# Early FFN weights in separate buffers, and another share-out of the low parts between VectorE, ScalarE and DMA

## The chip, the cores and the metric

One core of one Trainium2 chip runs the whole kernel. The metric is the time of one execution in microseconds of device time; the kernel before has a median of 1083.88 us over three runs. Every core has TensorE (PE, matrix products), VectorE (DVE), ScalarE (ACT), GpSimd (POOL) and SyncE (SP), each with its own instruction queue that is worked off in order, and DMA queues. Here SP issues the loads of weights, POOL issues the DMAs that add to their destination, ACT issues a few stores and loads of attention.

## What is computed

A hybrid encoder of two layers on 512 tokens of width 1024. Layer 0 mixes the tokens with a bidirectional gated linear attention (GLA), layer 1 with grouped-query softmax attention with 2-D rotary positions. Each is followed by a gated MLP with a width-3 convolution in it. Cut to what matters here:

```python
for i in range(DEPTH):                      # DEPTH = 2
    h = rmsnorm(x, norm_mix[i])
    x = x + (gla_mixer(h, ...) if i % 2 == 0 else attn_mixer(h, ...))
    x = x + conv_ffn(rmsnorm(x, norm_ffn[i]), ffn_w_up[i], ffn_w_conv[i], ffn_b_conv[i], ffn_w_down[i])

def conv_ffn(h, w_up, w_conv, b_conv, w_down):
    u = h @ w_up                            # 1024 -> 2 x 2816
    u = depthwise_conv3(u, w_conv) + b_conv
    val, gate = jnp.split(u, 2, axis=-1)
    return (jax.nn.silu(gate) * val) @ w_down
```

## The kernel before

**Two parts of each number.** All matrix products run on float32 numbers that are rounded to a shorter format (fp32r). So that nothing is lost, each operand is split into a high part (hi, the rounded number) and a low part (lo = number - hi), and each product is three matmuls: hi x hi, hi x lo and lo x hi. Every weight piece (128 x 1024 numbers, 512 KB) therefore goes through three steps: SP loads it into a `raw` buffer, ScalarE rounds it into `wh`, and VectorE subtracts to get `wl` (`split`, tiles `wh<-raw` on L353 and `wl<-raw,wh` on L354). A second way relieves VectorE (`low_dma`): ScalarE copies the raw piece into `wh` (L303) and a second time, times -1, into `wl` (L304), and rounds it on the way, so that `wl` is -hi; then POOL issues a DMA that adds the full number from memory (L342, in `flush`), so that `wl` becomes number - hi. A product that uses the piece waits for that DMA. Which pieces go which way is set by tables: `LOW_0` (up chunks whose first piece has its low part made by DMA), `STRIP_0` (the same for strips of the down projection), `Q_DMA` (pairs of activations).

**The FFN.** The 2816 hidden features are cut in 22 chunks of 128 (times value and gate). Chunks 4 to 21 (`SEVEN`) use a scheme of seven products instead of eight blocks (`seven_up`), in which some operands are sums of weight quarters. Such a chunk has four pieces h = 0 to 3 (`summed`). Piece 0 is loaded as it is; of the others, piece 2 (`e`, the `sum` tile) is a sum of quarters, made by VectorE (L324) from two loaded strips, or, for the chunks in `SUMS_DMA`, by a load and an accumulating DMA (`total`). The first matmul of a chunk that uses the low part of piece 0 is the row `r<-nh,wl`. The down projection comes in two parts, begun at chunks 9 and 17 (`DOWN_AFTER`), each with four strips of four pieces, and in a tail. `prepare` rounds and splits the activations of two neighbouring chunks, pair p (pair 6 is chunks 12 and 13), into four `gu` tiles; this runs some chunks behind TensorE, pair 6 while TensorE is at chunk 15.

**Order and buffers.** The instructions of each engine stand in the order that a scheduler gives them by priority, and a list of weight pieces (`W.todo`) decides what is loaded and rounded next. `W.ahead` and `W.piece` take from its front. Raw pieces go in a ring of five buffers (`NR`), `wh` and `wl` in rings of four. A larger set of buffers (`big`, 22 of them, shared with tiles of the mixers and the FFN) also exists. The first three up chunks of each layer (`EARLY`, six pieces) are rounded while the mixer before still works: the loop `early` calls `W.ahead(1)` at the steps of the output projection listed in `EARLY_AT`; their `wh` and `wl` lie in `big` buffers, their raw in the ring. In layer 1 those steps lie at the end of attention, where the last head's output is copied (`oT<-po`, hi on ACT L1465, lo on DVE L1466) and projected (`op<-oT,wh`, L578), and VectorE adds the result to `x` (L586).

Of the kernel before, what the change touches and what calls it, by code (L numbers as in the profile page):

```python
# [8 lines left out]
F32 = mybir.dt.float32  # L9
F32R = mybir.dt.float32r  # L10
U8 = mybir.dt.uint8
AF = mybir.ActivationFunctionType
# [3 lines left out]
S = 512  # L16
# [57 lines left out]
EARLY = 3  # L74
TOKENS_AT = (0, 4)
ROOT_AT = (1, 1)
EARLY_AT = (16, 17, 18, 20, 22, 24, 26, 28), (18, 19, 20, 22, 24, 26, 28, 30)
RANK = 0
PA = 4
LOADS = 3  # L80
SWITCH = 3
INPUT_AT = {1: (0, 1), 2: (2, 3)}
Q_DMA = (6,)
UP_DMA = (3,)
SUMS_DMA = (14, 15, 16)
SUMS_NEAR = 6
LOW_0 = (5, 6, 7, 8, 9, 15, 16, 17)
LOW_1 = ()
LOW_2 = ()
STRIP_0 = (0, 4, 8)  # L90
# [1 line left out]
NR = 5  # L92
# [19 lines left out]
def hybrid_encoder_kernel(  # L112
# [23 lines left out]
    pe, act, dve, pool, sync = nc.tensor, nc.scalar, nc.vector, nc.gpsimd, nc.sync  # L136
# [9 lines left out]
    def nm(s):  # L146
        uid[0] += 1
        return f"{s}{uid[0]}"
# [40 lines left out]
    class Weights:  # L189
# [2 lines left out]

        def __init__(self):
            self.todo, self.made, self.by_dma, self.pending = [], {}, [], []
            self.sums, self.last, self.fine = set(), None, []
            self.loaded, self.strip, self.vg, self.totals = {}, {}, {}, {}
            self.loads, self.wide, self.turn = LOADS, 0, 0

# [36 lines left out]
        def fetch(self, src, i, h):  # L235
            key = (id(src), i, h)
            if key in self.loaded:
                return self.loaded.pop(key)
            t = pair("raw", NR, F32, "raw")
            n = 2 if any(src is a and i < m for a, m in self.fine) else 1  # L240
            for q in range(n):
                w = 2 * S // n
                sync.dma_start(t[:, q * w : (q + 1) * w], src[i, :, h * 2 * S + q * w : h * 2 * S + (q + 1) * w])
            return t

        def load(self, key):
            src, i, h = key
# [17 lines left out]
        def make(self, key):  # L265
            src, i, h = key
            if i < 0:
                self.made[id(src), i, h] = self.make_vg(src, -i, h)
                return
            self.load(key)  # L270
            if (id(src), i) in self.sums:
                self.made[id(src), i, h] = self.summed(src, i, h)
                return
            r = self.loaded.pop((id(src), i, h))
            if i < EARLY and any(src is a for a in up):
                hi, lo = big(F32R, "wh"), big(F32R, "wl")
            else:
                hi, lo = self.two()
            if any(src is a and i < n for a, n in self.by_dma):
                self.low_dma(hi, lo, r)  # L280
            elif any(src is a and i in UP_DMA for a in up):
                self.low_dma(hi, lo, r, src[i, :, h * 2 * S : (h + 1) * 2 * S].bitcast(F32R))
            else:
                self.split(hi, lo, r, 2 if src is w_first else 1, src is w_first and i == 0 and h == 0)
            self.made[id(src), i, h] = (hi, lo)
# [4 lines left out]
        def total(self, src, i):  # L290
            if i in (SUMS_DMA if any(src is a for a in up) else TAIL_SUMS) and (id(src), i) not in self.totals:
                self.totals[id(src), i] = e = big(F32, "sum")
                sync.dma_start(e, src[i, :, : 2 * S])
                self.pending.append((e, src[i, :, S : 3 * S]))
# [5 lines left out]
            return pair("wh", NH, F32R, "wh"), pair("wl", NL, F32R, "wl")  # L300

        def low_dma(self, hi, lo, r, home=None):
            act.activation(hi, r, AF.Copy)  # L303
            act.activation(lo, r, AF.Copy, scale=-1.0)  # L304
            self.pending.append((lo, r if home is None else home))

        def summed(self, src, i, h):


            tiles = self.strip[id(src), i]  # L310
            r, t3, e = tiles if h == 0 else [tiles[h % 3]] + tiles[1:]
            if h == 3:
                del self.strip[id(src), i]
                r = t3[:, S:]
                dve.tensor_tensor(r, r, t3[:, :S], ALU.add)
                hi, lo = (sp.tile([P, S], F32R, tag="sq", bufs=3, name=nm(a)) for a in ("wh4", "wl4"))
                act.activation(hi, r, AF.Copy)
                self.last = dve.tensor_tensor(lo, r, hi.bitcast(F32), ALU.subtract)
                return hi, lo
            if h == 1:  # L320
                with tc.issue_after(self.last.ins) if self.last else ExitStack():
                    if e is None:
                        tiles[2] = e = pair("raw", NR, F32, "sum")
                        dve.tensor_tensor(fold(e), t3[:, :S].rearrange("p (o n) -> p o n", o=1).to_broadcast([P, 2, S]),  # L324
                                          fold(tiles[0]), ALU.add)
                    dve.tensor_tensor(t3[:, :S], e[:, S:], tiles[0][:, :S], ALU.add)
                tiles[0] = None
            hi, lo = self.two()
            low = (LOW_0, LOW_1, LOW_2) if any(src is a for a in up) else (STRIP_0, (), STRIP_2)
            if i in low[h]:  # L330
                self.low_dma(hi, lo, r)
                if h == 0:
                    self.pending[-1] = (fold(lo), self.outer(src, i).bitcast(F32R))
            else:
                self.split(hi, lo, r)
            return hi, lo
# [40 lines left out]
    W = Weights()  # L377
    up = [w_up[i] for i in range(2)]
    down_w = [w_down[i] for i in range(2)]

    def add_up(layer, chunks):
        for m in chunks:
            W.add(up[layer], (m,), 4 if m in SEVEN else 2)
            if m in SEVEN and m - 1 not in SEVEN and m - 1 not in DOWN_AFTER:
                W.todo[-5:-3] = W.todo[-4], W.todo[-5]

    def add_ffn(layer):
# [20 lines left out]
    W.todo += [(w_g, -i, half) for i in VG_ORDER for half in range(2)]  # L408
    W.todo += [(w_gout, n, half) for n, half in ((1, 1), (0, 1), (1, 0), (0, 0), (2, 1), (2, 0), (3, 1), (3, 0))]
    add_ffn(0)  # L410
    qk_order = [w_akq[i : i + 1] for i in range(w_akq.shape[0])]
    for a in qk_order[:2] + [w_av] + qk_order[2:] + [w_aout]:
        W.add(a)
    add_ffn(1)
    W.by_dma += [(w_kq, KQ_DMA)] + [(a, 1) for a in qk_order + [w_av]] + [(w_aout, 2)]


# [4 lines left out]
    raw = [big(F32, "xw") for _ in range(KC)]  # L422
# [177 lines left out]
    def early(osteps, first, layer):  # L600

        for n, _ in enumerate(osteps, first):
            if EARLY and n in EARLY_AT[layer]:
                W.ahead(1)

# [459 lines left out]
    def ffn(layer, norm, cw, nxt):  # L1065
# [136 lines left out]
        def prepare(p, y1, y2):  # L1202
# [9 lines left out]
            t4 = quads["half"]  # L1212
            far = p in Q_DMA
            split(y2, t[1], by_dma=far)
# [185 lines left out]
    def attention(norm, nxt):  # L1400
# [61 lines left out]
            return head, sc  # L1462

        def split(y, tile_):
            act.activation(tile_[:, :S], y, AF.Copy)  # L1465
            dve.tensor_tensor(tile_[:, S:], y, tile_[:, :S].bitcast(F32), ALU.subtract)  # L1466

        def whole(gen):
# [100 lines left out]
        def turn(h, i):  # L1569
# [6 lines left out]
            for c in range(2):  # L1576
# [34 lines left out]
        for t in range(len(blocks) + LAG2):  # L1611
# [122 lines left out]
```

## Time and profile before

| | |
|---|---|
| median of three runs | 1083.88 us (1082.36 to 1086.05) |
| profiled execution | 1083.11 us, of which the span of the profile is 1081.4 us |
| TensorE busy | 1066.0 us (99%) |
| VectorE busy | 940.7 us (87%) |
| ScalarE busy | 787.2 us (73%) |
| GpSimd busy | 162.4 us (15%) |
| TensorE clock granted | full in all 40 slices of the span |

A row of the timeline reads: start in us, duration in us, engine, line of the kernel, instruction, output tile <- input tiles, shape, count, and in brackets how long the engine had been idle and what ended that. The list of waits reads: engine, tile and line that waited, what it waited for; total us, how many times, the longest. An r tile is the result of a product of the FFN. Layer 0's FFN runs from about 220 to 550 us, layer 1's from about 737 us to the end.

### The profile page before, as it was taken

How to read it: one execution, taken by the hardware profiler on the slowest of the kernel's cores; microseconds unless marked ns; L12 is line 12 of the kernel's file. 1: busy time of each engine (PE TensorE's matmuls, PEld its weight loads, DVE VectorE, ACT ScalarE, POOL GpSimd, SP SyncE). 2: the span in 40 equal slices, each digit the busy share in tenths (PEclk: the TensorE clock that was granted, in tenths of full speed). 3: DMA queues.
4: the chain of work that ended last, by engine and by line, in shares of the span. 5: the costliest groups of instructions: out<-in, count | busy, mean ns of one | idle time of the engine just before them, and what ended most of it. 6: DMA issues, size and time to landing. Idle time of an engine off the chain costs nothing.

```text
span 1081.4 us, 18704 instructions
## 1 busy us (share of the span) xinstructions
PE 1066.0 (99%) x7176; PEld 980.4 (91%) x7176; DVE 940.7 (87%) x1415; ACT 787.2 (73%) x1260; POOL 162.4 (15%) x177
## 2 busy tenths in 40 slices
PE   9999999999999999999999999999999999999998
PEld 8788988788999999999988888778899999999997
DVE  7998968788999999999985588687899999999995
ACT  8679566658886779766784677675888677976783
POOL 0212112011101102010015333001101020201000
PEclk9999999999999999999999999999999999999999
DMA  8744446766555867474668475566756486756562
GB/s 303 186 127 106 120 141 219 243 138 136 139 145 129 217 170 157 129 174 121 218 171 200 126 195 156 166 217 173 140 144 144 125 202 184 161 137 149 145 195 79
DMA packets 76474, 176.41 MB, mean 163 GB/s; under 512 B 7008, under 2 KB 7776, under 8 KB 76384
## 3 DMA queue, kind: packets, MB, share of 16 engines
q1 hardware_dynamic: 50624, 114.23, 32.0%
q0 software_dynamic: 20864, 52.44, 27.7%
q10 hardware_dynamic: 4896, 8.55, 2.1%
q8 instruction: 56, 0.92, 0.3%
q14 instruction: 34, 0.28, 0.1%
HBM read 124.85 MB, written 14.68 MB: 129 GB/s over the span
## 4 chain that ended last, share of the span: by engine, by line
PE 43%; DMA 4%; issue 2%; DVE 2%; ACT 1%; POOL 0%; SPq 0%; DVEq 0%; ACTq 0%; POOLq 0%
PE r L1121 23%; PE op L578 3%; DMA wl<-in_w_down_dram 2%; PE up L526 1%; PE up L527 1%; PE up L525 1%; DMA wl<-in_w_up_dram 1%; PE av L552 1%; PE A L525 1%; PE A L526 1%; PE A L527 1%; PE B L527 1%; PE B L525 1%; PE B L526 1%; PE pt L1581 1%
## 5 line engine op out<-in xcount | busy, mean ns | idle before, releaser
L1121 PE MATMUL r<-xt,wh 128*128 128x256 f32 x1152 | 208.0, 282 | 0.0
L1121 PE MATMUL r<-gu,wh 128*128 128x256 f32 x1120 | 202.2, 283 | 0.7 <-ACT r L1337 0.7
L354 DVE TENSOR_TENSOR wl<-raw,wh 128x1024 fp32r<-128x1024 f32 x146 | 176.7, 1218 | 27.5 <-ACT wh L353 27.2
L353 ACT ACTIVATE wh<-raw 128x1024 fp32r<-128x1024 f32 x146 | 151.7, 1052 | 45.2 <-DMA raw<-in_w_up_dram 10.4
L1121 PEld LDWEIGHTS r<-xt,wh 128*128 128x128 f32 x1152 | 178.9, 190 | 0.2
L1121 PEld LDWEIGHTS r<-gu,wh 128*128 128x128 f32 x1120 | 173.7, 190 | 1.9 <-ACT r L1337 1.1
L1121 PE MATMUL r<-xt,wl 128*128 128x256 f32 x576 | 162.9, 283 | 0.0
L1121 PE MATMUL r<-gu,wl 128*128 128x256 f32 x560 | 157.6, 283 | 0.6 <-DMA wl<-in_w_down_dram 0.6
L1121 PE MATMUL r<-nh,wl 128*128 128x256 f32 x432 | 122.7, 284 | 3.9 <-DMA wl<-in_w_up_dram 3.8
L1121 PE MATMUL r<-nh,wh 128*128 128x256 f32 x432 | 122.1, 283 | 0.0
L1121 PE MATMUL r<-nl,wh 128*128 128x256 f32 x432 | 121.6, 281 | 0.0
L1121 PEld LDWEIGHTS r<-xt,wl 128*128 128x128 f32 x576 | 109.7, 191 | 0.0
L1121 PEld LDWEIGHTS r<-gu,wl 128*128 128x128 f32 x560 | 106.3, 190 | 1.0 <-DMA wl<-in_w_down_dram 1.0
L1121 PEld LDWEIGHTS r<-nh,wl 128*128 128x128 f32 x432 | 82.0, 190 | 5.1 <-DMA wl<-in_w_up_dram 5.1
L1121 PEld LDWEIGHTS r<-nh,wh 128*128 128x128 f32 x432 | 82.0, 190 | 0.2
L1121 PEld LDWEIGHTS r<-nl,wh 128*128 128x128 f32 x432 | 82.1, 190 | 0.1
L578 PE MATMUL op<-oT,wh 128*128 128x512 f32 x256 | 73.5, 395 | 1.0 <-DVE x L586 0.8
L354 DVE TENSOR_TENSOR wl<-sum,wh 128x1024 fp32r<-128x1024 f32 x56 | 68.2, 1218 | 4.9 <-ACT wh L353 4.9
L353 ACT ACTIVATE wh<-sum 128x1024 fp32r<-128x1024 f32 x56 | 59.1, 1055 | 16.4 <-DVE sum L324 11.4
L303 ACT ACTIVATE wh<-raw 128x1024 fp32r<-128x1024 f32 x46 | 48.4, 1052 | 19.0 <-PE A L526 6.3
L324 DVE TENSOR_TENSOR sum<-raw,raw 128x1024 f32<-128x1024 f32 x50 | 60.9, 1217 | 1.2 <-issue 1.2
L578 PEld LDWEIGHTS op<-oT,wh 128*128 128x128 f32 x256 | 47.3, 188 | 11.8 <-DVE x L586 1.2
(314 smaller groups left out, 2584.1 us busy)
## 6 DMA issues: line engine op xcount, KB each, us to landing
raw<-in_w_up_dram SPq DMA_DIRECT2D x78, 512.0 KB, 5.0
raw<-in_w_down_dram SPq DMA_DIRECT2D x44, 512.0 KB, 4.6
wl<-raw POOLq DMA_DIRECT2D x20, 512.0 KB, 5.0
wl<-in_w_up_dram POOLq DMA_DIRECT2D x20, 512.0 KB, 5.9
ring<-p ACTq DMA_DIRECT2D x32, 256.0 KB, 2.6
xw<-in_xw_dram SPq DMA_DIRECT2D x8, 512.0 KB, 6.9
raw<-in_w_v_dram SPq DMA_DIRECT2D x8, 512.0 KB, 5.4
raw<-in_w_g_dram SPq DMA_DIRECT2D x8, 512.0 KB, 4.2
```

What stands on the lines that cost most here:

```text
L303: act.activation(hi, r, AF.Copy)
L324: dve.tensor_tensor(fold(e), t3[:, :S].rearrange("p (o n) -> p o n", o=1).to_broadcast([P, 2, S]), fold(tiles[0]), ALU.add)
L353: act.activation(hi[:, sl], a, AF.Copy)
L354: dve.tensor_tensor(lo[:, sl], a, hi[:, sl].bitcast(F32), ALU.subtract)
L525: mm(ps, wh, mh, start=start, stop=False, **kw)
L526: mm(ps, wh, ml, start=False, stop=False, **kw)
L527: return mm(ps, wl, mh, start=False, stop=stop, **kw)
L552: mm(ps[j][:, :width], hl[k][i == 2][:, j * P : (j + 1) * P], (wl if i == 1 else wh)[:, sl], start=k == 0 and i == 0, stop=k == KC - 1 and ...
L578: mm(pss[ng][n], wt[:, sl], mv, start=k == late[0][0] and i == 0, stop=k == late[-1][-1] and i == 2)
L1121: mm(dst, w[:, sl], m, start=start and j == 0 and a == 0, stop=j == len(pairs) - 1 and a == 2, skip_group_check=True)
L1581: pe.transpose(tp[:, k, j * P : (j + 1) * P].bitcast(F32R), ps[j][:, o : o + P], identr)
```

## The change

It has five parts. Line numbers shift by up to 32: L303 and L304 become L324 and L323, L342 becomes L363, L353 and L354 become L374 and L375, L1465 becomes L1497, L1163 becomes L1195.

1. The raw pieces of the three early chunks are loaded in `big` buffers by `load_early`, at steps of their own (`LOAD_AT`), and their SP instructions are ordered behind the last ordinary load (`W.queued`). They are rounded at six steps instead of eight; each rounding is ordered behind the latest copy of an attention split (`W.behind`), where there is one.
2. `low_dma` makes the scaled copy first, and hi second, for all pieces that use it.
3. `Q_DMA` is empty: the four low parts of pair 6 are made by VectorE.
4. `SUMS_DMA` is cut from chunks 14, 15, 16 to 16: VectorE makes the sums of 14 and 15.
5. `LOW_0` gains chunks 12, 13, 14, whose first piece's low part now comes by DMA; all pieces on these tables get a higher priority (`LOW_RANK`).

`lead` does nothing here, since `LEADS` is empty.

```diff
-EARLY_AT = (16, 17, 18, 20, 22, 24, 26, 28), (18, 19, 20, 22, 24, 26, 28, 30)
+EARLY_AT = (18, 20, 22, 24, 26, 28), (18, 20, 22, 24, 26, 28)
+LOAD_AT = ((12, 13, 14, 16, 18, 20), (13, 14, 15, 16, 17, 18))
+BEHIND = 1
+LOW_RANK = 20
-Q_DMA = (6,)
+Q_DMA = ()
-SUMS_DMA = (14, 15, 16)
+SUMS_DMA = (16,)
-LOW_0 = (5, 6, 7, 8, 9, 15, 16, 17)
+LOW_0 = (5, 6, 7, 8, 9, 12, 13, 14, 15, 16, 17)
...
-            t = pair("raw", NR, F32, "raw")
+            t = big(F32, "raw") if self.early(src, i) else pair("raw", NR, F32, "raw")
...
+            if not self.early(src, i):
+                self.queued = start
             return t
+        def early(self, src, i):
+            return i < EARLY and any(src is a for a in up)
+        def load_early(self):
+            for src, i, h in self.todo:
+                if self.early(src, i) and (id(src), i, h) not in self.loaded:
+                    with tc.issue_after(self.queued.ins):
+                        return self.load((src, i, h))
...
-            if i < EARLY and any(src is a for a in up):
+            if self.early(src, i):
                 hi, lo = big(F32R, "wh"), big(F32R, "wl")
-            else:
-                hi, lo = self.two()
+                with tc.issue_after(self.behind.ins) if BEHIND and self.behind else ExitStack():
+                    self.split(hi, lo, r)
+                self.made[id(src), i, h] = (hi, lo)
+                return
+            hi, lo = self.two()
...
         def low_dma(self, hi, lo, r, home=None):
+            act.activation(lo, r, AF.Copy, scale=-1.0)
             act.activation(hi, r, AF.Copy)
-            act.activation(lo, r, AF.Copy, scale=-1.0)
...
-                self.low_dma(hi, lo, r)
+                with tc.high_priority(LOW_RANK) if LOW_RANK else ExitStack():
+                    self.low_dma(hi, lo, r)
...
+            if EARLY and n in LOAD_AT[layer]:
+                W.load_early()
             if EARLY and n in EARLY_AT[layer]:
                 W.ahead(1)
...
-            act.activation(tile_[:, :S], y, AF.Copy)
+            W.behind = act.activation(tile_[:, :S], y, AF.Copy)
```

ScalarE's queue about chunk 17 of layer 0 before: `wh_4603` is the hi and `wl_4604` the scaled copy of the chunk's first piece, `wh_4527` the hi of a piece of chunk 16, the `gu` rows are the end of pair 6, and `r_4600` a result of chunk 15 that ScalarE copies.

```order
L304 ACTIVATE gu_4438<-y_4301 128x512
L303 ACTIVATE gu_4440<-q_4434 128x512
L304 ACTIVATE gu_4440<-q_4434 128x512
L1190 ACTIVATE u_4620<-r_4602 128x512
L303 ACTIVATE gu_4441<-b_4448 128x256
L304 ACTIVATE gu_4441<-b_4448 128x256
L353 ACTIVATE wh_4527<-raw_4383 128x1024
L1178 ACTIVATE y_4577<-r_4398,cw 128x512
L1163 ACTIVATE r_4600<-r_4547 128x256
L1182 ACTIVATE y_4521<-y_4521 128x512
L303 ACTIVATE wh_4603<-raw_4531 128x1024
```

```order
L1190 ACTIVATE r_4676<-r_4652 128x512
L317 ACTIVATE wh_4584<-raw_4383 128x512
L304 ACTIVATE wl_4604<-raw_4531 128x1024
L1178 ACTIVATE y_4648<-u_4620,cw 128x512
L1178 ACTIVATE y_4706<-r_4547,cw 128x512
```

The same place after the change: the scaled copy is `wl_4600`, its hi `wh_4599`, the hi of chunk 16's piece `wh_4523`.

```order
L324 ACTIVATE wh_4599<-raw_4527 128x1024
L1214 ACTIVATE y_4517<-y_4517 128x512
L1195 ACTIVATE r_4596<-r_4543 128x256
L374 ACTIVATE wh_4523<-raw_4384 128x1024
L323 ACTIVATE wl_4600<-raw_4527 128x1024
L1222 ACTIVATE r_4672<-r_4648 128x512
L337 ACTIVATE wh_4580<-raw_4384 128x512
```

The scaled copies of pair 6 (L304, `gu`) are gone from the queue, and the copy `wl` stands ahead of the r and wh rows (L1190 and L317 before) that it followed.

ScalarE's queue at the end of layer 1's attention before: `wh_8089`, `wh_8108`, `wh_8144` and `wh_8162` are early pieces, `wh_7913`, `wh_8038` and `wh_8063` weights of the attention's output projection, `oT_7938` and `oT_7974` the outputs of the last two heads.

```order
L353 ACTIVATE wh_7913<-raw_7467 128x1024
L353 ACTIVATE wh_8089<-raw_8042 128x1024
L1465 ACTIVATE oT_7938<-po_7870 128x512
L1584 ACTIVATE pth_7889<-pt_7941 128x2x256
L1584 ACTIVATE pth_7891<-pt_7948 128x2x256
L353 ACTIVATE wh_8038<-raw_7781 128x1024
L353 ACTIVATE wh_8108<-raw_8067 128x1024
L353 ACTIVATE wh_8144<-raw_8080 128x1024
L1465 ACTIVATE oT_7974<-po_7961 128x512
L353 ACTIVATE wh_8162<-raw_8093 128x1024
L353 ACTIVATE wh_8063<-raw_7860 128x1024
```

And after the change, with `oT_7934` and `oT_7970` as the outputs and `wh_8104`, `wh_8138`, `wh_8154` as the early pieces:

```order
L374 ACTIVATE wh_7909<-raw_7463 128x1024
L1497 ACTIVATE oT_7934<-po_7866 128x512
L1616 ACTIVATE pth_7885<-pt_7937 128x2x256
L1616 ACTIVATE pth_7887<-pt_7944 128x2x256
L374 ACTIVATE wh_8043<-raw_7777 128x1024
L1497 ACTIVATE oT_7970<-po_7957 128x512
L374 ACTIVATE wh_8104<-raw_7985 128x1024
L374 ACTIVATE wh_8138<-raw_7994 128x1024
L374 ACTIVATE wh_8154<-raw_8022 128x1024
L374 ACTIVATE wh_8072<-raw_7856 128x1024
```

Three early pieces that stood ahead of the second oT copy, the first of them ahead of the first copy too, now stand behind both.

POOL's queue of accumulating DMAs from chunk 12 of layer 0 on, before (`sum` rows are sums of chunks 14, 15, 16, `wl` rows low parts of chunks 15, 16, 17 and of a down strip, `gu` rows low parts of pair 6):

```order
L342 DMA sum_4010<-in_w_up_dram 128x1024
L342 DMA sum_4141<-in_w_up_dram 128x1024
L342 DMA sum_4286<-in_w_up_dram 128x1024
L342 DMA wl_4328<-in_w_up_dram 128x2x512
L342 DMA wl_4477<-in_w_up_dram 128x2x512
L342 DMA gu_4439<-y_4428 128x512
L342 DMA gu_4438<-y_4301 128x512
L342 DMA gu_4440<-q_4434 128x512
L342 DMA gu_4441<-b_4448 128x256
L342 DMA wl_4604<-in_w_up_dram 128x2x512
L342 DMA wl_4749<-in_w_down_dram 128x2x512
```

And after, from the same place:

```order
L363 DMA wl_3921<-in_w_up_dram 128x2x512
L363 DMA wl_4050<-in_w_up_dram 128x2x512
L363 DMA wl_4195<-in_w_up_dram 128x2x512
L363 DMA sum_4285<-in_w_up_dram 128x1024
L363 DMA wl_4327<-in_w_up_dram 128x2x512
L363 DMA wl_4473<-in_w_up_dram 128x2x512
L363 DMA wl_4600<-in_w_up_dram 128x2x512
L363 DMA wl_4745<-in_w_down_dram 128x2x512
```

Three low parts (chunks 12, 13, 14) came in, two sums and pair 6's four rows went out.

More of the change, by code (lines that the diff above doesn't have):

```diff
@@ L76 @@
 ROOT_AT = (1, 1)
-EARLY_AT = (16, 17, 18, 20, 22, 24, 26, 28), (18, 19, 20, 22, 24, 26, 28, 30)
+EARLY_AT = (18, 20, 22, 24, 26, 28), (18, 20, 22, 24, 26, 28)
+LOAD_AT = ((12, 13, 14, 16, 18, 20), (13, 14, 15, 16, 17, 18))
+BEHIND = 1
+LEAD = 0
+LEADS = ()
 RANK = 0
+LOW_RANK = 20
 PA = 4
@@ L194, in __init__ @@
             self.todo, self.made, self.by_dma, self.pending = [], {}, [], []
-            self.sums, self.last, self.fine = set(), None, []
+            self.sums, self.last, self.fine, self.behind = set(), None, [], None
             self.loaded, self.strip, self.vg, self.totals = {}, {}, {}, {}
@@ L242, in fetch @@
                 w = 2 * S // n
-                sync.dma_start(t[:, q * w : (q + 1) * w], src[i, :, h * 2 * S + q * w : h * 2 * S + (q + 1) * w])
-            return t
+                start = sync.dma_start(t[:, q * w : (q + 1) * w],
+                                       src[i, :, h * 2 * S + q * w : h * 2 * S + (q + 1) * w])
+            if not self.early(src, i):
+                self.queued = start
+            return t
+        def early(self, src, i):
[5 more added lines that the diff above has]
+                        return self.load((src, i, h))
         def load(self, key):
@@ L385, in add_up, with lead @@
                 W.todo[-5:-3] = W.todo[-4], W.todo[-5]
+    def lead(layer):
+        for m in LEADS:
+            key = (up[layer], m, 0)
+            at = next(n for n, k in enumerate(W.todo) if k[0] is key[0] and k[1:] == key[1:])
+            W.todo.pop(at)
+            W.todo.insert(at - LEAD, key)
     def add_ffn(layer):
@@ L410, in hybrid_encoder_kernel @@
     add_ffn(0)
+    lead(0)
     qk_order = [w_akq[i : i + 1] for i in range(w_akq.shape[0])]
@@ L414, in hybrid_encoder_kernel @@
     add_ffn(1)
+    lead(1)
     W.by_dma += [(w_kq, KQ_DMA)] + [(a, 1) for a in qk_order + [w_av]] + [(w_aout, 2)]
```

## The prediction

> **What bounds the kernel now.** I read the page first, then the waits of TensorE, then the timeline of single engines around each wait. The busy line and the waits:
>
> ```profile
> PE 1066.0 (99%) x7176; PEld 980.4 (91%) x7176; DVE 940.7 (87%) x1415; ACT 787.2 (73%) x1260; POOL 162.4 (15%) x177
> PE r L1121 <- DMA wl<-in_w_up_dram: 3.8, 4, 1.7
> PE po L525 <- DVE oT L1466: 1.0, 1, 1.0
> PE op L578 <- DVE x L586: 0.8, 1, 0.8
> PE r L1121 <- DMA wl<-in_w_down_dram: 0.6, 2, 0.3
> ```
>
> TensorE is busy for 1066.0 of 1081.4 us. The change takes no matmul away, so all it can win is idle time of TensorE, and the four waits above are those that it touches. Each place in the timeline of PE (start, duration, tile, idle before it in brackets; x2 is two instructions drawn as one row):
>
> ```profile
> 200.79 0.50 PE L578 MATMUL op<-oT,wh 128*128 128x512 f32 x1 [0.81 <-DVE x L586]
> 412.99 0.39 PE L1121 MATMUL r<-nh,wl 128*128 128x256 f32 x1 [0.20 <-DMA wl<-in_w_up_dram]
> 434.99 0.39 PE L1121 MATMUL r<-nh,wl 128*128 128x256 f32 x1 [1.69 <-DMA wl<-in_w_up_dram]
> 525.10 0.40 PE L1121 MATMUL r<-gu,wh 128*128 128x256 f32 x2
> 525.75 0.39 PE L1121 MATMUL r<-gu,wl 128*128 128x256 f32 x1 [0.25 <-DMA wl<-in_w_down_dram]
> 706.66 0.47 PE L525 MATMUL po<-pth,vh 128*128 128x512 f32 x1 [0.97 <-DVE oT L1466]
> 712.78 0.50 PE L578 MATMUL op<-oT,wh 128*128 128x512 f32 x1 [0.19 <-DVE oT L1466]
> 830.25 0.39 PE L1121 MATMUL r<-nh,wl 128*128 128x256 f32 x1 [0.54 <-DMA wl<-in_w_up_dram]
> 930.48 0.28 PE L1121 MATMUL r<-nl,wh 128*128 128x256 f32 x1
> 930.88 0.39 PE L1121 MATMUL r<-nh,wl 128*128 128x256 f32 x1
> 952.56 0.39 PE L1121 MATMUL r<-nh,wl 128*128 128x256 f32 x1 [1.38 <-DMA wl<-in_w_up_dram]
> 1043.42 0.39 PE L1121 MATMUL r<-gu,wl 128*128 128x256 f32 x1 [0.34 <-DMA wl<-in_w_down_dram]
> ```
>
> The bracket understates the loss. Two r matmuls in one row of 0.40 start 0.12 apart, so the row at 525.10 has its second start at 525.22; the next is due at 525.34 and comes at 525.75: 0.41 lost where the bracket says 0.25. I add that 0.16 to each bracket; the row at 930.88 has none, but starts 0.40 after the one at 930.48, 0.28 too late. In layer 0: 0.97 at 200; 0.36 (chunk 15), 1.85 (chunk 17) and 0.41 (down strip 8) in the FFN. In layer 1: 1.13 and 0.35 at the end of attention; 0.70 (chunk 9), 0.28, 1.54 and 0.50 in the FFN. Together 8.1 us, the most that the change can win here. Nearly half is chunk 17 (434.99 and 952.56).
>
> **The low parts that come by DMA, lo ahead of hi.** Chunk 15, then chunk 17, on ACT and POOL, before:
>
> ```profile
> 402.68 0.36 ACT L1163 ACTIVATE r<-r 128x256 f32<-128x256 f32 x1
> 405.62 1.05 ACT L304 ACTIVATE wl<-raw 128x1024 fp32r<-128x1024 f32 x1
> 406.96 1.08 POOL L342 DMA_DIRECT2D wl<-in_w_up_dram  x1 [7.02 <-PE r L1121]
> 420.15 0.62 ACT L304 ACTIVATE gu<-q 128x512 fp32r<-128x512 f32 x1
> 424.20 1.05 ACT L303 ACTIVATE wh<-raw 128x1024 fp32r<-128x1024 f32 x1
> 425.14 0.59 ACT L1190 ACTIVATE r<-r 128x512 f32<-128x512 f32 x1
> 425.66 0.62 ACT L317 ACTIVATE wh<-raw 128x512 fp32r<-128x512 f32 x1
> 426.18 1.05 ACT L304 ACTIVATE wl<-raw 128x1024 fp32r<-128x1024 f32 x1
> 427.52 1.08 POOL L342 DMA_DIRECT2D wl<-in_w_up_dram  x1 [4.50 <-PE r L1121]
> wl<-in_w_up_dram POOLq DMA_DIRECT2D x20, 512.0 KB, 5.9
> ```
>
> The scaled copy ends, POOL issues 0.3 us later, and the piece lands 5.9 us after that (median), and 7.4 for chunk 17: 434.95 less 427.52. TensorE begins with it at once, so a copy that ends x earlier ends the wait x earlier, up to its size. Chunk 15's copy now stands just ahead of the r at 402.68, some 2.6 us earlier than 405.62, against 0.36 to win. Chunk 9 and the down strip 8 move in the same way, by at least the one hi copy (1.05), against 0.41 to 0.70. All five of these small waits go: 0.36 + 0.41 + 0.70 + 0.28 + 0.50 = 2.25, of which I take 2.2; below zero they can hardly come out, since only hi is later, by one copy, and hi is ready without a DMA.
>
> Chunk 17's lo stays behind its hi in the new order. It gains from two things: four scaled copies of pair 6 (the gu row is one; three of 0.52 pitch and one of 0.31, 1.87 in all) no longer stand ahead of it on ScalarE, and the rows at 425.14 and 425.66 (1.04) are now behind it. At best it ends at 427.23 - 2.91 = 424.3, at worst, if the wl buffer that it writes is not free sooner, where it does now. Its use without a wait would be at 433.14, so it needs 1.85 (1.54 in layer 1). I take 1.5 earlier, the middle of 0 and 2.91: 0.35 stays in layer 0 and 0.04 in layer 1, gain 3.0 of 3.39. The bounds are 0 and 3.39. Pair 6's four DMAs leave POOL's queue and the DMA engines just ahead of this piece; should its flight fall from 7.4 to the median 5.9, all 3.39 come, and I count nothing for that.
>
> The Trainium skill (DMA: Bandwidth & Descriptors, section Anatomy of one DMA) prices a DMA of this queue at about 2.0 us plus bytes over 436 GB/s, an estimate of 3.2 us for 512 KB. By it every piece would land before its use today and chunk 17 would win all 3.39, for a sum of 7.1 instead of 6.7 and a time of 1076.8; this trace's 5.9 and 7.4 us disagree, and the sum goes by them.
>
> **The swaps between VectorE, ScalarE and POOL.** Per layer:
>
> ```profile
> L354 DVE TENSOR_TENSOR wl<-raw,wh 128x1024 fp32r<-128x1024 f32 x146 | 176.7, 1218 | 27.5 <-ACT wh L353 27.2
> L324 DVE TENSOR_TENSOR sum<-raw,raw 128x1024 f32<-128x1024 f32 x50 | 60.9, 1217 | 1.2 <-issue 1.2
> L318 DVE TENSOR_TENSOR wl<-raw,wh 128x512 fp32r<-128x512 f32 x56 | 38.4, 686 | 6.3 <-PE r L1121 4.3 <-ACT wh L317 1.7
> ```
>
> VectorE loses three low parts of chunks 12 to 14 (-3 x 1.22), gains two sums for chunks 14 and 15 (+2 x 1.22) and the four low parts of pair 6 (3 x 0.69 and a half-size one, about 0.4): +1.25 us per layer. ScalarE gains three copies of 1.05 (the row at 405.62) and loses pair 6's, about +1. POOL issues three DMAs more and six fewer, SP two loads fewer. ScalarE has room (73%); POOL too. The new pieces of chunks 12 to 14 are made in the way of chunks 5 to 8, none of which appears among the waits: no cost. VectorE is where it can hurt. Its busy time in two stretches from chunk 13 on (length, then busy us), its largest idle time there, and the first piece of the second down part with its use:
>
> ```profile
> 395.00:415.00 20.00, 19.88 (x31) 1.00 0.67 169
> 415.00:445.00 30.00, 27.64 (x44) 1.00 0.76 160
> 422.85 1.23 DVE L354 TENSOR_TENSOR wl<-raw,wh 128x1024 fp32r<-128x1024 f32 x1 [1.33 <-ACT wh L353]
> 446.96 1.23 DVE L354 TENSOR_TENSOR wl<-raw,wh 128x1024 fp32r<-128x1024 f32 x1 [0.32 <-ACT wh L353]
> 449.39 0.28 PE L1121 MATMUL r<-gu,wl 128*128 128x256 f32 x1
> ```
>
> VectorE has 2.48 us free in these 50 us. That piece is ready at 448.19, 1.20 before its use. After the change TensorE arrives 0.36 + 1.5 = 1.9 sooner and VectorE has 1.25 more to do; with all its idle time used the piece has 1.20 + 2.48 - 1.9 - 1.25 = 0.5 in hand, with none used it is 1.95 late. I take 0.4 late in each layer, nearer the first end, since the largest idle stretch (1.33) waited for ScalarE, which pair 6 now frees: -0.8 in all, with 0 and 3.9 as bounds.
>
> **The early weights.** ScalarE and VectorE at the end of layer 1's attention, then at the end of layer 0's GLA; the last row is VectorE's busy time (6.05 of 10) after layer 1's attention:
>
> ```profile
> 703.59 1.06 ACT L353 ACTIVATE wh<-raw 128x1024 fp32r<-128x1024 f32 x1 [2.94 <-DMA raw<-in_w_up_dram]
> 705.83 0.68 DVE L1466 TENSOR_TENSOR oT<-po,oT 128x512 fp32r<-128x512 f32 x1
> 194.95 2.01 ACT L353 ACTIVATE wh<-raw 128x1024 fp32r<-128x1024 f32 x2 [1.78 <-DMA raw<-in_w_up_dram]
> 200.06 1.27 DVE L586 TENSOR_TENSOR x<-x,op 128x512 f32<-128x512 f32 x2
> 730.00:740.00 10.00, 6.05 (x10) 1.00 0.94 254
> ```
>
> ScalarE stood 2.94 us on a raw piece of the FFN with the attention's oT copy behind it, and TensorE at 706.66 waited for that oT. In the new order both oT copies go ahead of those pieces, and the load starts earlier: 1.13 and 0.35 go; I take 1.4 of 1.48. In layer 0 the same kind of wait (1.78) pushed VectorE's x add to 200.06, which TensorE awaited; with the raw loads in their own buffers I take 0.9 of 0.97. Either could turn out as zero if the big buffers come free late, or gain a little more. SP issues the early pieces sooner, behind the last load of the attention; the ring's own loads follow them as now. What is late next: up to three more roundings (1.05 on ScalarE, 1.22 on VectorE each) fall behind the attention, where VectorE is idle for 3.95 of the 10 us from 730, ahead of their first use. I cost them at nothing; that cover gone they cost at most 3 x 1.22 = 3.7.
>
> **Sum.** 2.2 + 3.0 - 0.8 + 1.4 + 0.9 = 6.7 us. The profiled execution took 1083.11 us (span 1081.4), the median of the runs is 1083.88, 0.8 above it. 1083.88 - 6.7 = 1077.2, rounded to 1077.0 for the flight of chunk 17's piece.
>
> **Rivals.**
> A. VectorE becomes the bound from chunk 14 to the second down part, and what chunk 17 wins is waited for there. For it: 19.88 of 20 us busy. Against: three low parts leave it just ahead. Then 3.9 rather than 0.8 is given back, the sum is 3.6: 1080.3.
> B. The change does not do what it says for the low parts: chunk 17's lo waits for its buffer and lands as late as now. Against: ACT is 1.87 us lighter ahead of it. Gain 2.2 + 2.3 (the early weights): with chunk 17 no earlier the 1.9 of A is not lost either, so nothing is given back: 4.5, 1079.4. With the early loads failing too (the big buffers come free late), 2.2: 1081.7.
> C. The other side: the sums for chunks 14 and 15 and pair 6's low parts (4.9 us per layer) come where VectorE has nothing left, while the three that leave (3.7) are freed too early to help. Past the 2.48 of idle time and the 1.2 in hand this decides: each piece from chunk 15 on is late by the rest, and since every chunk's gate work goes through the same queue, ScalarE and POOL follow late and chunk 17's wait returns in full. 4.9 - 1.2 = 3.7 per layer if no idle time is usable, 7.4 in all, against 2.3 kept from the early weights, the low parts' gains lost: 1089.0. With the 2.48 us of idle time used it is 1.2 per layer: 1084.0.
>
> **Chances.** My forecast (1075 to 1079.5) 0.60; A 0.15; B 0.16 with its worse form; C 0.09. A difference under 0.3% (3.25 us) is what a measurement here can't tell from none. Faster by more: the first, two thirds of A and half of B, less a little, 0.76; within: 0.18; slower: two thirds of C, 0.06. The range takes in the forecast, A and B, from 1074.5 (all 8.1 us and a little beside) to 1082.5.
>
> **What would show it.** In the waits of PE after the change, "wl<-in_w_up_dram" falls from 3.8 to under 0.8 and "wl<-in_w_down_dram", "oT" and "x" vanish; PE's busy time stays near 1066. If A or C holds, there are new waits of r for DVE wl (L375) between chunk 14 and the first strips of the second down part, and VectorE shows 10 of 10 us busy there. If B holds, the idle of 1.4 to 1.7 before the first r<-nh,wl of chunk 17 is still there. New waits of xhl or up after the attention would make the early weights the wrong step. Not covered: a wait in stages that I have not costed, from the new order of matmuls.

## The result and the profile after

| | before | after |
|---|---|---|
| median | 1084.84 us (1082.36 to 1086.05, 4 runs) | 1076.06 us (1075.65 to 1076.42, 4 runs) |
| ratio | | 0.9922, 95% interval 0.9902 to 0.9942 |
| profiled execution, its span | 1083.11, 1081.4 us | 1076.42, 1074.7 us |

The change makes the kernel faster by 0.8%. Between the two profiled executions the difference is 6.7 us, as the sum had it; the fourth run of the kernel before lifted its median, so the medians differ by 8.8. In the other jobs below the kernel before has medians of 1083.45 to 1084.19, and a run there whose program is the changed one (behind_0) is 7.0 us under it.

The busy line, then the waits of TensorE (total, times, longest), after:

```profile
PE 1064.9 (99%) x7176; PEld 981.2 (91%) x7176; DVE 938.1 (87%) x1421; ACT 788.9 (73%) x1258; POOL 159.9 (15%) x171
PE pt L1613 <- DMA ring<-p: 1.1, 1, 1.1
PE r L1153 <- ACT r L1369: 0.7, 1, 0.7
PE r L1153 <- ACT r L1299: 0.6, 2, 0.3
```

All four waits that the prediction spoke of are gone: no r waits for a low part by DMA, no po for oT, no op for x. One kind is new, r for ScalarE's r on L1299, twice. The wait for the ring of the attention (L1613), 0.6 before, is 1.1; the r for L1369 stood there before too, as L1337. Chunk 17 after, on ScalarE, POOL, the DMA issues and TensorE:

```profile
423.34 1.05 ACT L323 ACTIVATE wl<-raw 128x1024 fp32r<-128x1024 f32 x1
424.69 1.07 POOL L363 DMA_DIRECT2D wl<-in_w_up_dram  x1 [10.93 <-ACT wl L323]
wl<-in_w_up_dram POOLq DMA_DIRECT2D x1, 512.0 KB, 6.7
431.69 0.28 PE L1153 MATMUL r<-nl,wh 128*128 128x256 f32 x1
431.81 0.28 PE L1153 MATMUL r<-nh,wl 128*128 128x256 f32 x1
```

From issue to use are 7.12 us without any wait (431.81 less 424.69), where before there were 7.47 with 1.85 of waiting in them, so 5.62. The copy comes 1.5 us earlier against TensorE, as assumed, and the flight was 6.7 instead of 7.4. The piece has about 0.4 us in hand. The new wait, and its cause on ScalarE and VectorE:

```profile
447.75 0.69 DVE L335 TENSOR_TENSOR raw<-raw 128x512 f32<-128x512 f32 x1
448.48 0.63 ACT L337 ACTIVATE wh<-raw 128x512 fp32r<-128x512 f32 x1 [1.92 <-DVE raw L335]
449.01 0.37 ACT L1299 ACTIVATE r<-r 128x256 f32<-128x256 f32 x1
449.43 0.39 PE L1153 MATMUL r<-gu,wh 128*128 128x256 f32 x1 [0.30 <-ACT r L1299]
395.00:415.00 20.00, 20.00 (x30) 1.00 0.79 188
415.00:445.00 30.00, 29.65 (x48) 1.00 0.53 126
```

VectorE has 0.35 us free of 50 (2.48 before). At the first strip of the second down part it makes a sum late (447.75); ScalarE stands 1.92 us on it with the small copy of r behind, and TensorE waits for that copy: 0.30 and the 0.16 that a bracket leaves out, 0.46 in each layer. At the end of the GLA and of attention, after:

```profile
199.82 0.68 DVE L616 TENSOR_TENSOR x<-x,op 128x512 f32<-128x512 f32 x1
200.14 0.39 PE L608 MATMUL op<-oT,wh 128*128 128x512 f32 x1
200.36 0.39 PE L608 MATMUL op<-oT,wl 128*128 128x512 f32 x1
200.59 0.39 PE L608 MATMUL op<-oT,wh 128*128 128x512 f32 x1
700.41 0.60 ACT L1497 ACTIVATE oT<-po 128x512 fp32r<-128x512 f32 x1 [2.49 <-PE po L557]
705.72 2.95 ACT L374 ACTIVATE wh<-raw 128x1024 fp32r<-128x1024 f32 x3
```

ScalarE now waits for TensorE's po and copies oT at once; the early pieces (three in the row at 705.72) follow. At 200 VectorE's add comes hardly earlier (200.06 before), yet TensorE doesn't wait. Its order is another: two groups of three matmuls of the projection more stand ahead of the one that needs the add. At 0.23 us each the six take 1.4 us, and the wait was 0.97.

### The profile page after: what moved, and what is told of

Read it like the earlier page. It is cut to its first block, busy times and chain, and to the rows that moved or that the text cites. A ratio compares the mean times of both kernels' runs of the same rounds, so it can differ in the third digit from the quotient of the medians.

```text
span 1074.7 us, 18675 instructions
## 1 busy us (share of the span) xinstructions
PE 1064.9 (99%) x7176; PEld 981.2 (91%) x7176; DVE 938.1 (87%) x1421; ACT 788.9 (73%) x1258; POOL 159.9 (15%) x171
## 4 chain that ended last, share of the span: by engine, by line
PE 89%; DVE 8%; ACT 1%; issue 1%; DMA 0%; DVEq 0%; ACTq 0%
PE r L1153 46%; PE op L608 8%; PE vg L733 5%; PE up L556 3%; PE up L555 3%; PE up L557 3%; PE kq L665 2%; DVE wl L375 2%; PE av L582 1%; PE A L555 1%; PE A L556 1%; PE A L557 1%; PE B L557 1%; PE B L555 1%; PE B L556 1%; PE pt L1613 1%
## 5 line engine op out<-in xcount | busy, mean ns | idle before, releaser
L375 DVE TENSOR_TENSOR wl<-raw,wh 128x1024 fp32r<-128x1024 f32 x140 | 168.8, 1216 | 18.8 <-ACT wh L374 18.4
L374 ACT ACTIVATE wh<-raw 128x1024 fp32r<-128x1024 f32 x140 | 145.2, 1052 | 35.6 <-DVE raw L346 7.0
L374 ACT ACTIVATE wh<-sum 128x1024 fp32r<-128x1024 f32 x56 | 59.2, 1058 | 23.1 <-DVE sum L344 17.0
L375 DVE TENSOR_TENSOR wl<-sum,wh 128x1024 fp32r<-128x1024 f32 x56 | 68.2, 1218 | 4.2 <-ACT wh L374 4.2
L363 POOL DMA_DIRECT2D wl<-in_w_up_dram x26 | 27.4, 1055 | 266.3 <-ACT wl L323 166.4
L324 ACT ACTIVATE wh<-raw 128x1024 fp32r<-128x1024 f32 x52 | 54.7, 1052 | 16.5 <-PE A L556 6.7
L344 DVE TENSOR_TENSOR sum<-raw,raw 128x1024 f32<-128x1024 f32 x54 | 65.7, 1216 | 0.0
```

What stands on the lines that cost most here:

```text
L363: pool.dma_start(lo.bitcast(F32) if same else lo, r, accum_op=ALU.add)
L374: act.activation(hi[:, sl], a, AF.Copy)
L375: dve.tensor_tensor(lo[:, sl], a, hi[:, sl].bitcast(F32), ALU.subtract)
```

## The experiments

The first four undo one part of the changed kernel each, to see which wait comes back.

### Early weights undone: no_early

```diff
-EARLY_AT = (18, 20, 22, 24, 26, 28), (18, 20, 22, 24, 26, 28)
-LOAD_AT = ((12, 13, 14, 16, 18, 20), (13, 14, 15, 16, 17, 18))
-BEHIND = 1
+EARLY_AT = (16, 17, 18, 20, 22, 24, 26, 28), (18, 19, 20, 22, 24, 26, 28, 30)
+LOAD_AT = ((), ())
+BEHIND = 0
-            t = big(F32, "raw") if self.early(src, i) else pair("raw", NR, F32, "raw")
+            t = pair("raw", NR, F32, "raw")
```

> The changed kernel with only the early weights undone: their raw pieces are loaded into the ring again, rounded at the old eight steps, not held behind the attention's copies. Theory: TensorE's waits for VectorE's x at the end of the GLA (0.97 us) and for oT at the end of attention (1.1 and 0.35) return, and the wait for the ring of attention falls from 1.27 back to 0.8; no wait of an FFN chunk for a low part returns. 1076.1 + 2.0 = 1078.1. Rival: those waits went because scaled copies come first (also for the attention's output weights) and not because of the buffers: then they stay away and the time is 1076.

Measured 1079.9 us, ratio to before 0.9955 (0.994 to 0.997). The waits, a row of ScalarE, and the add and a matmul at the end of the GLA:

```profile
PE po L555 <- DVE oT L1498: 1.0, 1, 1.0
PE ms L541 <- DVE sq L533: 0.5, 1, 0.5
701.90 1.06 ACT L374 ACTIVATE wh<-raw 128x1024 fp32r<-128x1024 f32 x1 [2.92 <-DMA raw<-in_w_up_dram]
199.93 0.69 DVE L616 TENSOR_TENSOR x<-x,op 128x512 f32<-128x512 f32 x1
200.66 0.40 PE L608 MATMUL op<-oT,wh 128*128 128x512 f32 x1
```

The attention's wait is back, with ScalarE 2.92 us on a raw piece as before, and a wait of 0.5 at the start of the FFN beside it (ms). The wait for the ring stays at 1.1, where 0.8 was expected. The GLA's wait for x is not there: the matmul at 200.66 runs without one. That doesn't clear the early weights, though. TensorE's 192 matmuls of that projection stand in the order of the kernel before again; it begins them at 173.05 instead of 171.93, having lost the time in the first 90 us, and so comes to the matmul that waited (200.90 here) after the add, which ends at 200.62. This part pays, by more than was expected (3.8 us, not 2.0).

### hi first again: hi_first

```diff
+            act.activation(hi, r, AF.Copy)
             act.activation(lo, r, AF.Copy, scale=-1.0)
-            act.activation(hi, r, AF.Copy)
```

> The changed kernel with only the order in low_dma undone: hi first, then the scaled copy. Theory: the small waits of chunk 9, chunk 15 and down strip 8 return in both layers (2.4 us together before), chunk 17 in part, by up to the one hi copy (1.05 per layer): 1078.5 to 1080.5. Rival: the higher priority of these copies and the missing copies of pair 6 had already moved them far enough: 1076 to 1076.8.

Measured 1077.69 us (1077.55 to 1077.83), ratio 0.9934 (0.9918 to 0.9951).

```profile
PE r L1153 <- DMA wl<-in_w_down_dram: 0.7, 2, 0.4
PE r L1153 <- DMA wl<-in_w_up_dram: 0.5, 1, 0.5
424.27 1.07 POOL L363 DMA_DIRECT2D wl<-in_w_up_dram  x1 [9.68 <-ACT wl L324]
431.40 0.28 PE L1153 MATMUL r<-nh,wl 128*128 128x256 f32 x1
```

The down strips (two) and chunk 9 of layer 1 wait again; chunks 15 and 17 do not. Chunk 17's issue stands 7.13 us ahead of its use, as in the changed kernel. Neither side had the time: the loss is 1.6 us by the medians of the two jobs.

### Pair 6 by DMA again: pair6_by_dma

```diff
-Q_DMA = ()
+Q_DMA = (6,)
```

> The changed kernel with only pair 6's low parts by DMA again (four scaled copies on ScalarE and four DMAs per layer, 2.5 us less on VectorE). Theory: these copies and DMAs, which stood just ahead, were what made chunk 17's piece late: its wait returns, 1 to 1.85 per layer, the wait of r for ScalarE at the first strip of the second down part (0.46 per layer) goes: 1077.1 to 1078.9. Rival: the scaled copy ahead of hi is enough for chunk 17: no DMA wait, and the 0.46 goes too: 1075.2.

Measured 1074.5 us (1074.35 to 1075.35), ratio 0.9906 (0.9891 to 0.9921): the fastest kernel of this study. The changed one's four runs, and the four of behind_0, are all above this kernel's four, though they come from other jobs and the intervals of the ratios overlap. Outside the GLA two waits of size are left, neither of them in a chunk; the last two rows are chunk 17's copies:

```profile
PE pt L1613 <- DMA ring<-p: 1.2, 1, 1.2
PE r L1153 <- ACT r L1369: 0.7, 1, 0.7
422.25 1.05 ACT L323 ACTIVATE wl<-raw 128x1024 fp32r<-128x1024 f32 x1
424.38 1.05 ACT L324 ACTIVATE wh<-raw 128x1024 fp32r<-128x1024 f32 x1
```

The rival was right: here the scaled copy does stand ahead of its hi. In the changed kernel pair 6's copies and DMAs do not make chunk 17 late, and moving them to VectorE bought nothing and cost the 0.46 per layer.

### Low parts of chunks 12 to 14 back on VectorE: no_low12to14

```diff
-LOW_0 = (5, 6, 7, 8, 9, 12, 13, 14, 15, 16, 17)
+LOW_0 = (5, 6, 7, 8, 9, 15, 16, 17)
```

> The changed kernel with the low parts of chunks 12 to 14 back on VectorE (3.65 us more there per layer, three copies and three DMAs fewer). Theory: VectorE has almost nothing left from chunk 13 on, so this is paid in new waits of r for VectorE's or ScalarE's pieces in chunks 12 to 17 and the second down part, 1 to 3 us per layer: 1078 to 1082. Rival: VectorE still has room, since pieces are made one or two ahead: 1076 to 1077, with the wait at the first strip no larger than 0.46 + 0.5.

Measured 1083.0 us, ratio 0.999 (0.9979 to 1.0001): 6.9 us lost for 3.65 us of VectorE work per layer.

```profile
PE r L1153 <- DMA wl<-in_w_up_dram: 3.0, 3, 1.9
PE r L1153 <- ACT wh L374: 1.5, 2, 0.8
PE r L1153 <- ACT r L1299: 1.4, 2, 0.7
413.13 0.38 PE L1153 MATMUL r<-nh,wl 128*128 128x256 f32 x1 [0.85 <-DMA wl<-in_w_up_dram]
930.87 0.38 PE L1153 MATMUL r<-nh,wl 128*128 128x256 f32 x1 [1.87 <-DMA wl<-in_w_up_dram]
```

This is close to rival C: with VectorE late, ScalarE's copies are late, and the waits for DMA return, at chunk 15 in both layers and chunk 16 in layer 0. Not at chunk 17, which rival C named: its issue is 5.82 us ahead of the use, and the piece flew 5.8. The sums and pair 6 on VectorE are paid for by these three low parts.

The next four ask what moved chunk 17's copy, since neither its order nor pair 6 did by itself.

### The priority alone: rank_0

```diff
-LOW_RANK = 20
+LOW_RANK = 0
```

> The changed kernel with LOW_RANK 0: the scaled copies get no higher priority. Open after the first runs: neither hi first nor pair 6 by DMA brought back the wait of chunk 17, so what moved its copy 1.5 us earlier? Theory: the three low parts of chunks 12 to 14 that left VectorE did; the priority does nothing: no wait of r for a low part, 1075.6 to 1076.6. Rival: the priority did: the wait of chunk 17 returns with 0.5 to 1.5 per layer, 1077 to 1079.

Measured 1076.64 us (1076.25 to 1077.06), ratio 0.9937 (0.9921 to 0.9954), with no wait for a low part. The priority moves a few rows of ScalarE and does nothing that can be measured. Whether the three low parts moved the copy, as the theory says, this run doesn't show.

### Sums of chunks 14 and 15 by DMA again: sums_by_dma

```diff
-SUMS_DMA = (16,)
+SUMS_DMA = (14, 15, 16)
```

> The changed kernel with the sums of chunks 14 and 15 by DMA again (2.43 us less on VectorE, two DMAs more per layer). Theory: VectorE is the limit in this stage, so the wait of r for ScalarE at the first strip of the second down part (0.46 per layer) goes, and the low parts land no later: 1075.1. Rival: two more accumulating transfers lengthen the flights of chunks 15 to 17, whose slack is 1.3, 1.6 and 0.45 us: waits for DMA wl of 0.5 to 1 us per layer, 1076.5 to 1078.

Measured 1077.41 us (1075.48 to 1079.65), ratio 0.9944 (0.9928 to 0.996). Two DMA issues near chunk 12, and two rows of TensorE:

```profile
sum<-in_w_up_dram POOLq DMA_DIRECT2D x1, 512.0 KB, 10.3
wl<-in_w_up_dram POOLq DMA_DIRECT2D x1, 512.0 KB, 10.3
382.83 0.39 PE L1153 MATMUL r<-nh,wh 128*128 128x256 f32 x1 [0.67 <-ACT r L1195]
895.06 0.39 PE L1153 MATMUL r<-nh,wl 128*128 128x256 f32 x1 [0.72 <-DMA wl<-in_w_up_dram]
```

Both theories hold in part. The wait on L1299 is gone. But the sum of chunk 14 (issued at 366.44) and the new low part of chunk 12 (370.33) are in flight together, and TensorE waits at chunk 12. It is the low part that is slower for it: 10.3 us here against 6.9 in the changed kernel, while that sum takes 10.1 in the kernel before with no low part beside it. The rival named chunks 15 to 17; it is the place where the two lists meet. The profile is of the fastest of the four runs (1075.48), so what the others lost beside it stays open.

### Chunks 12 to 14 alone on the kernel before: only_low12to14

```diff
-LOW_0 = (5, 6, 7, 8, 9, 15, 16, 17)
+LOW_0 = (5, 6, 7, 8, 9, 12, 13, 14, 15, 16, 17)
```

> The kernel before with chunks 12 to 14 added to LOW_0 and nothing else. Theory: this alone removes the wait of chunk 17 (1.85 and 1.54), since VectorE's backlog in chunks 12 to 14 held up what ScalarE does ahead of the copy; the waits of chunk 9, down strip 8, attention and the GLA stay: 3.4 us under the kernel before, ratio 0.9969. Rival: it takes the order or pair 6 as well: ratio 0.999 to 1.

Measured 1084.52 us, ratio 1.0009 (0.9993 to 1.0024). The theory fell.

```profile
PE r L1121 <- DMA wl<-in_w_up_dram: 3.4, 4, 1.1
```

Chunk 17's waits shrink (1.85 to 0.94, 1.54 to 0.21), but chunk 12 waits in both layers (1.10 the longer), with the sum of chunk 14 in flight beside it as in the run before: its low part takes 9.9 and 10.5 us. Here these low parts gain nothing; with fewer sums by DMA, in the changed kernel, they are worth 6.9 us (no_low12to14).

### The early weights alone: only_early

Edit: the changed kernel with hi first, pair 6 and three sums by DMA, the old `LOW_0` and no priority.

> The kernel before with the early weights' part of the change alone (big raw buffers, load and rounding steps, rounding behind the attention's copies). Theory: the waits at the end of the GLA (0.97) and of attention (1.24 and 0.35) go, those of the FFN stay: 2.4 us under the kernel before, ratio 0.9978. Rival: the wait at the end of the GLA, which did not return when this part was undone, stays: 1.5 us under, ratio 0.9986.

Measured 1080.33 us, ratio 0.9967 (0.9956 to 0.9978). The waits for oT and x are both gone; those for the low parts of chunk 9, chunk 17 and (0.9 in all) the down strips are there:

```profile
PE r L1153 <- DMA wl<-in_w_up_dram: 3.9, 3, 1.8
```

So this part does cure the GLA's wait. Every kernel here that has it has the six matmuls more ahead of the one that needs the add, and no wait. The kernels without it have the old order, and all wait (0.6 to 0.9), except no_early, where TensorE came late.

The last four: lo first alone, lo first with pair 6, a repetition, and a step further.

### lo first alone on the kernel before: only_lo_first

```diff
-            act.activation(hi, r, AF.Copy)
             act.activation(lo, r, AF.Copy, scale=-1.0)
+            act.activation(hi, r, AF.Copy)
```

> The kernel before with the scaled copy ahead of hi, nothing else. Theory: the small waits of chunk 9, chunk 15 and down strip 8 go (2.4 us together), chunk 17 keeps most of its wait (its hi stays ahead): ratio 0.9975. Rival: the copies wait for their buffers and come no earlier: ratio 0.999 or more.

Measured 1078.38 us, ratio 0.9953 (0.9939 to 0.9968): two lines swapped gain 5.1 us, where the changed kernel's program gains 7.0 in the same job (behind_0).

```profile
PE r L1121 <- DMA wl<-in_w_up_dram: 0.4, 2, 0.2
423.52 1.06 ACT L303 ACTIVATE wl<-raw 128x1024 fp32r<-128x1024 f32 x1
424.87 1.08 POOL L342 DMA_DIRECT2D wl<-in_w_up_dram  x1 [2.83 <-ACT wl L303]
425.51 1.05 ACT L304 ACTIVATE wh<-raw 128x1024 fp32r<-128x1024 f32 x1
```

Here the scaled copy of chunk 17 simply took the place of its hi, and hi the place of the copy. Its issue stands 7.60 us ahead of the use (5.62 before), and chunk 17 does not wait in either layer. Chunk 15 keeps its two waits of 0.2 us: its scaled copy starts at 404.96, still behind its hi (400.35), and the issue is 5.67 us ahead of the use, as before. A wait of 0.7 at the start of layer 1's FFN (ms) is new.

### lo first and pair 6: lo_first_and_pair6

Edit: as the last, with `Q_DMA = ()`.

> The kernel before with the scaled copy ahead of hi and pair 6's low parts on VectorE. The prediction gave these two as what moves chunk 17's copy 1.5 us earlier. If so, the wait of chunk 17 falls to 0 to 0.35 per layer with VectorE's added 2.5 us per layer as the only price: ratio 0.9945 to 0.996. Rival, after the first runs: the copy also needs VectorE relieved of the low parts of chunks 12 to 14; then 1 us or more per layer stays at chunk 17, or returns as waits of r for pieces of VectorE and ScalarE: ratio 0.9965 to 0.999.

Measured 1079.19 us (1078.43 to 1081.33), ratio 0.9958 (0.9942 to 0.9975). No wait of 0.2 us or more for a low part is left. At the end of attention and behind it, in the profile of the slowest of the four runs:

```profile
PE po L525 <- DVE oT L1466: 1.0, 1, 1.0
PE ms L511 <- DVE sq L503: 0.9, 1, 0.9
```

The wait of the attention is that of the kernel before; the one behind it (ms) is in only_lo_first too. The time is in the theory's range. Next to only_lo_first, in the same job, pair 6 gains nothing, although chunk 17's copy comes 0.5 us earlier.

### The ordering behind the attention's copies: behind_0

```diff
-BEHIND = 1
+BEHIND = 0
```

> The changed kernel with BEHIND 0: early raw pieces in the large buffers and loaded at their own steps, but their rounding is free to stand ahead of the attention's oT copies. Theory: the buffers let the loads start early enough that ScalarE no longer stands on them: oT waits stay away, 1076. Rival: only the order saves the end of attention, since in layer 1 these loads start at 696 us, when the copies are due: the oT wait (0.5 to 1.2) returns, 1076.6 to 1077.8.

This edit moves no instruction on any engine, so the run is a repetition of the changed kernel: 1076.46 us beside 1076.06. The ordering does nothing by itself; the buffers and steps put the roundings there. The wait for the ring is 0.8 us in this profile and 1.1 in the first one of the same program, so of the 0.5 us that it seemed to have grown, 0.3 is within its own scatter.

### Pair 6 by DMA and all sums on VectorE: pair6_by_dma_sums_0

```diff
-Q_DMA = ()
-SUMS_DMA = (16,)
+Q_DMA = (6,)
+SUMS_DMA = ()
```

> The fastest so far (pair 6 by DMA again) with the sum of chunk 16 on VectorE too: one more accumulating transfer of 8 to 9 us flight leaves the DMA engines, 1.22 us per layer go to VectorE. Theory (VectorE had just become free enough): VectorE's load is then that of the changed kernel, and about 0.2 to 0.5 us per layer returns as a wait of r for ScalarE at the first strip of the second down part: 1074.9 to 1075.5. Rival: the lighter DMA load gains more (chunk 17 lands earlier, no wait appears): 1074.5 or less.

Measured 1075.64 us (1075.11 to 1076.08), ratio 0.9928 (0.9913 to 0.9942).

```profile
432.55 0.39 PE L1153 MATMUL r<-nh,wl 128*128 128x256 f32 x1 [0.76 <-DMA wl<-in_w_up_dram]
```

One sum more on VectorE per layer costs 1.1 us by the medians of the two jobs, whose runs overlap (up to 1075.35 without it, from 1075.11 with it). The wait does not come back at the first strip but at chunk 17. Its copy is late again in both layers (6.15 and 6.14 us from issue to use); layer 1 escapes by its flight of 5.8 instead of 7.0.

### Chunk 17 across the kernels

From the same rows in each profile, layer 0: POOL's issue to TensorE's use (less what TensorE waited), and the flight.

| kernel | issue to use, us | flight, us |
|---|---|---|
| before | 5.62 | 7.4 |
| only_low12to14 | 5.91 | 6.8 |
| no_low12to14 | 5.82 | 5.8 |
| pair6_by_dma_sums_0 | 6.15 | 7.0 |
| after | 7.12 | 6.7 |
| hi_first | 7.13 | 6.6 |
| only_lo_first | 7.60 | 6.8 |
| lo_first_and_pair6 | 8.11 | 5.7 |
| pair6_by_dma | 8.12 | 6.0 |
| sums_by_dma | 9.63 | 5.8 |

Where work is taken from VectorE, the copy comes earlier than in the changed kernel: by 1.0 us in pair6_by_dma, by 2.5 in sums_by_dma. Where work is given to it, the copy comes later: by 1.3 us in no_low12to14, and by 2.0 in pair6_by_dma_sums_0 against pair6_by_dma. On the kernel before it isn't so: with pair 6 on VectorE the copy comes 0.5 us earlier (lo_first_and_pair6 against only_lo_first), and with the low parts of chunks 12 to 14 taken away only 0.3. That VectorE's backlog sets when the copy is made is therefore a likely reading of the changed kernel, not shown: the order of ScalarE's queue changes from kernel to kernel too, and no run parts the two.

## Why the prediction was right, and where not

- **The bound and the sum.** Only waits of TensorE could be won, 8.1 us at most. Forecast 6.7 and 1077.0; measured 1076.06, and 6.7 between the profiled executions. That the two agree to the tenth is partly luck: by the rows the five terms come to 7.2 (2.25 + 3.39 - 0.92 + 1.48 + 0.97), and the ring's wait, which was not in the sum, is 0.5 longer. The medians' 8.8 is above the bound, 7.0 in the job of behind_0 below it: the two jobs differ by more than some of the terms weighed here.
- **The five small waits (2.2).** All are gone. hi_first shows that the order of the copies cured chunk 9 and the down strips. Chunk 15 is another matter, and there the forecast had the wrong reason: the swap alone leaves its issue 5.67 us ahead of the use, as before. The low parts of chunks 12 to 14 by DMA make it 7.55 (only_low12to14).
- **Chunk 17 (3.0, bounds 0 and 3.39).** All 3.39 came. The move of 1.5 us was sized rightly, and the flight shortened too, which I had left out. The step that failed is the reason: I gave the gain to pair 6's four copies on ScalarE, 1.87 us, and to two rows that fall behind the copy. pair6_by_dma puts pair 6's copies back, and the scaled copy comes earlier still; next to only_lo_first, taking them away moves it by 0.5 us. lo first alone is enough (only_lo_first), and without it the rest of the change is enough (hi_first). I had read from the new order that lo "stays behind its hi" and so gains nothing by the swap. In the changed kernel that holds (7.13 us from issue to use with hi first, 7.12 with lo first); on the kernel before the swap exchanges the two places. Either cure suffices, so undoing one shows nothing; it took the parts alone to see it. Which part of the rest cures it in hi_first is open: the low parts of chunks 12 to 14 alone leave 0.94 and 0.21, and pair 6 alone was not run.
- **VectorE's price (-0.8).** Measured -0.92, twice 0.46, at the place named, the first strip of the second down part. But it came as a wait for ScalarE's r behind a wh that stood on a late sum, not for VectorE's low part. Rival A did not happen; pair6_by_dma shows the price was there to be saved. no_low12to14 shows how near rival C was: without the three low parts that leave, 6.9 us are lost.
- **The early weights (1.4 and 0.9).** At the attention right in place and cause: no_early brings back ScalarE's 2.92 us on a raw piece and the wait behind it. The three roundings that now follow cost nothing, as said. At the GLA the wait went, and by this part, but not for the reason given: the add is only 0.24 us earlier, and it is TensorE's order that changed, with six more matmuls ahead of the one that needs the add. The part as a whole is worth more than the 2.3 of the sum: 3.8 us undone (no_early), 3.9 alone (only_early).
- **The page's rule.** 3.2 us, an estimate by the Trainium skill's formula (DMA: Bandwidth & Descriptors, section Anatomy of one DMA), against 5.7 to 7.4 for the piece of chunk 17 in layer 0 of these profiles: the trace decides. By the rule there would have been no wait at chunk 17 to win, not one that is won in full.

Not run: lo first and the early weights together without any swap between engines. Alone they gain 5.1 and 3.9 us, so if these add up, the two would do as well as the changed kernel.

## What to carry to other kernels

Where a piece needs two preparations and only one of them starts a transfer, do that one first: this alone gave 5.1 us of 1084. Before moving work between two engines that feed each other, ask which of them is behind in that stage. In the changed kernel ScalarE is busy 73% of the span and for 42.6 of the 50 us from 395, yet its rounding at 448.48 stood 1.92 us on VectorE, which had 0.35 us free. When a wait has gone, see whether the instruction that waited comes later, before you call it cured (no_early). Undo each part alone and also run each part alone, since two sufficient cures hide each other.

## What the runs showed of the hardware that was not expected

The low part of chunk 17, 512 KB by an accumulating DMA, takes 5.7 to 7.4 us from issue to landing in layer 0 of these kernels. The low part of chunk 12 takes 9.9 to 11.0 with the sum of chunk 14 in flight beside it (sums_by_dma and only_low12to14, both layers), and 6.9 and 7.4 in the changed kernel without that. Two in flight are not always slow: in the changed kernel chunk 14's low part (391.82) and chunk 16's sum (393.43) overlap and take 7.2 and 9.0. Two profiles of one program differ by 0.3 us in a single wait for DMA (ring, 1.1 and 0.8).
